# Full-array last tiles in an attention and DFT kernel: zero padding of keys, shift rows and DFT rows, and stores issued behind the next table's load

## The chip, the cores and the metric

The kernel runs on one core of a Trainium2 chip. The metric is the device time of one execution in microseconds (us), as the median of several executions. TensorE (PE) does the matrix products; its weight loads are shown apart as PEld. VectorE (DVE), ScalarE (ACT) and GpSimd (POOL) work on elements, and the SyncE queue (SP) issues most of the loads and stores.

## The reference

One encoder layer over 4096 tokens and 16 meta tokens put in front of them (4112 rows, model width 1024). After an RMS norm one projection gives the input of a Fourier branch, its gate, queries (8 heads of 64), keys and values (2 heads of 64) and an attention gate:

```
u = rmsnorm(h, norm_g)
f_in, f_gate, q, k, v, a_gate = split(u @ w_in)
f_out = (real(fft2(f_in over positions and 64 channels, ortho)) @ w_fmix + b_fmix) * silu(f_gate)
a_out = softmax(rope(norm(q)) @ rope(norm(k)).T / 8) @ v * silu(a_gate)
h = h + concat(f_out, a_out) @ w_out
out = rmsnorm(h, final_g)[16:]
```

All arithmetic is fp32 in the reference. The kernel reaches its accuracy with pairs of 16-bit numbers (a high part and a remainder), so that a projection takes three matmuls instead of one.

## The kernel before

**Phase A** (`phase_a`) makes the RMS statistics, the projections of 33 row tiles (tile 32, `NT`, holds the 16 meta rows), and the folded inputs of the position DFT. `proj` takes eight chunks of the model width, and for each the three products xh·wh, xh·wl and xl·wh (`mm3`, lines 84 to 86).

**Phase B** (`phase_b`) is the attention sweep. There are 8 blocks of 512 queries and 4 head pairs in each, so 32 "pairs" (b, p). A pair is a stream of 66 steps j: two heads times 33 key tiles. A step has two halves. `qk` multiplies one key tile with the 512 queries (L1031 the high part, L1032 the rest, in which the row shift sits as extra rows), ACT takes the exponential (L1035), and POOL or DVE subtracts its bfloat16 part (`rr`, L1037). `pvm`, four steps later, multiplies the probabilities with the values in nine matmuls (L1052 to L1059). In the last key tile of a head only 16 meta keys exist: `n = P if t < NT else NMETA`, so its two `qk` matmuls have 16 columns of weights and its nine `pvm` matmuls 16 rows. After it ACT copies the sum (L1063) and POOL does four operations on `ob` (L1067 to L1070).

Between the halves of the steps the sweep carries other work. Two matmuls with 64 rows per shift unit (`grp`, L962) find a row maximum for the next pair; DVE reduces them (L963). At step 63 `fin` (L993) transposes the shift row `nm`, 32 columns wide, and DVE spreads it into `qB` (L998) for the next pair. From the fifth pair on, the output projection of the block before (L1112) takes steps 14 to 61.

The position DFT is done in 17 units of 128 output rows for each of two parities (`dft_units`): 51 matmuls each, against a table `ct` of 1088 KB that `ct_load` fetches; the table pool has two buffers. Unit 16 holds the four rows left over, so its matmuls have four columns of weights, and its table of both parities is 68 KB. The first seven or so units run ahead of the sweep, up to 18 matmuls between two shift units (`f_step`); the others run inside the first pairs, three matmuls per step. A unit's end is `gather` (ACT copies the sum), and behind it `mix` applies the map and the gate; `mix` ends with POOL's product into `mo` (L869) and with the stores to `mf_d` (L872). While the first block runs, `block0` also fetches the output projection's weights (`wot`, L943) and splits them into `woh` (ACT) and `wol` (DVE), one chunk in seven steps from step `W0 = 234` on.

SP works in order: a store that waits for `mo` holds up every load written behind it. PE too takes its instructions strictly in the order in which they are written.

Of the kernel before, what the change touches and what calls it, by code (L numbers as in the profile page):

```python
# [32 lines left out]
P = 128  # L33
# [21 lines left out]
def emit(tc, a):  # L55
# [4 lines left out]
    with top:  # L60
# [39 lines left out]
        cts = []  # L100
# [26 lines left out]
def phase_a(tc, a, pool, mm3, id16, id32, sc):  # L127
# [15 lines left out]
    with ExitStack() as st:  # L143
# [150 lines left out]
        def proj(t, c0, c1):  # L294
# [3 lines left out]
            for d in range(ND):  # L298
                mm3(o, xh[:, d, :n], xl[:, d, :n], wh[:, d, c0:c1], wl[:, d, c0:c1], d == 0, d == ND - 1)
# [326 lines left out]
        wsplit(*GB, 3)  # L626
        tile_tr(NT)
        tile_gate(31, 768, fg_d)
# [43 lines left out]
def phase_b(tc, a, pool, mm3, id32, id16, sc):  # L672
# [10 lines left out]
    with ExitStack() as st:  # L683
# [14 lines left out]
        nm = [bp.tile([P, 32], F16, name=f"nm{i}") for i in range(2)]  # L698
# [60 lines left out]
        def dft_units(u, ty, spare):  # L759
# [3 lines left out]
            o, m = (0, P) if u < 16 else (4 * ty, 4)  # L763
# [3 lines left out]
            def one(*args):  # L767
# [4 lines left out]
                r = ps[0][:m, cs]  # L772
                if i == 8:
                    T.matmul(r, ct[0:96, x, 16, o:o + m], src[0:96, 8, 0, cs], start=False, stop=True,
                             skip_group_check=True)
                else:
                    T.matmul(r, ct[:, x, 2 * i + (w == 2), o:o + m], src[:, i, int(w == 1), cs],  # L777
# [5 lines left out]
            def gather():  # L783
                rows = slice(0, P) if u < 16 else slice(32 * ty, 32 * ty + 4)
                sk = stk if u < 16 else stk8
                c = ps[0][:m]
# [8 lines left out]
        behind = []  # L795
# [51 lines left out]
        def mix(u, early):  # L847
# [53 lines left out]
        def f_step(n, heavy, early=False):  # L901

            while flist:
# [49 lines left out]
        def max_units(i):  # L953
# [29 lines left out]
            def red():  # L983
                m = sm.tile([P, 4, 2], F32, tag="mm", name="mm")
                V.tensor_reduce(m, mx, axis=AX.X, op=ALU.max)
                V.scalar_tensor_tensor(out=n[:, 0:8].rearrange("p (e s)->p e s", s=4),
# [38 lines left out]
        def step(h, kv, t, qa, qb, acc, ob, gate):  # L1025
            n = P if t < NT else NMETA
            d = {}

            def qk(eng):
                s = pq.tile([P, 512], F32, tag="s", name="s")  # L1030
                T.matmul(s[:n], K[kv][:, t, 0, :n], qa, start=True, stop=False)  # L1031
                T.matmul(s[:n], K[kv][:, t, 1, :n], qb, start=False, stop=True)  # L1032
                pe = wk.tile([P, 512], F32, tag="pe", name="pe")
                rr = wk.tile([P, 512], F16, tag="rr", name="rr")
                S.activation(pe[:n], s[:n], AF.Exp, scale=HD ** -0.5)  # L1035
                hi = pe.bitcast(BF16)[:, 1::2]
                eng.tensor_tensor(out=rr[:n], in0=pe[:n], in1=hi[:n], op=ALU.subtract)  # L1037
                d["hi"], d["rr"] = hi, rr

            def pvm():  # L1040
# [6 lines left out]
                vh, va, vl = VV[:n, t, kv, :65], VV[:n, t, kv], VV[:n, t, kv, 65:129]  # L1047
# [415 lines left out]
```

## Time and profile before

| | |
|---|---|
| median of 3 runs | 3327.89 us (3327.48 to 3328.08) |
| profiled execution | 3325.33 us, of which the span shown is 3323.5 us |
| TensorE's granted clock, mean | 0.996 |
| PE busy | 3261.9 us (98%) |
| DVE, POOL, ACT busy | 71%, 68%, 51% |
| phase A, tables and first shift units, sweep | about 0 to 728, to 812, to the end |

A line of a timeline gives start, duration, engine, line, operation, output<-inputs and shape, and in brackets how long the engine was idle before and what released it. For matmuls "128\*16" is rows \* columns of the weights. Matmuls overlap in the pipeline: the distance from one start to the next says what a matmul costs, not the duration shown. A matmul streams its columns (512 in L1031) at 2.4 GHz when the granted clock is 1.00; 512 columns are 0.21 us.

### The profile page before, as it was taken

Reading aid. Unit: us, or ns where it says so; the run is one execution under the profiler, and the core shown is the slowest. Engines: PE = TensorE matmul, PEld = TensorE weight load, DVE = VectorE, ACT = ScalarE, POOL = GpSimd, SP = SyncE. Lnnn points to the kernel's source line nnn. Section 1 sums busy time; section 2 is a strip of 40 time slices with the busy share of each in tenths; the row PEclk is TensorE's granted clock in tenths of the full one; section 3 lists DMA queues with packets and bytes.
Section 4 is the critical chain, followed back from the end, with each engine's and each line's share of the span. In section 5 each row is a group of like instructions: output and inputs, shape, how many; then the busy total and the mean of one; then the engine's idle time right before and its main releaser. Section 6 shows DMA issues by size and latency. Waiting matters only on the chain.

```text
span 3323.5 us, 78632 instructions
## 1 busy us (share of the span) xinstructions
PE 3261.9 (98%) x33109; PEld 1888.5 (57%) x33109; DVE 2368.1 (71%) x3225; ACT 1703.8 (51%) x2967; POOL 2273.9 (68%) x2168
## 2 busy tenths in 40 slices
PE   8999999998999999999999999999999999999998
PEld 4555555556666555555555555555555555555554
DVE  6766565536666877777777777777777777777764
ACT  5443444333555555555555555555555555555553
POOL 3655555425777777777777777777777777777762
PEclk9999999999999999999999999999999999999999
DMA  6444444347422110110001000110100010000001
GB/s 220 145 164 134 140 150 133 102 151 212 131 91 65 66 53 23 36 45 21 21 21 46 21 20 24 49 33 21 46 21 21 20 46 21 24 29 28 21 21 58
DMA packets 142296, 223.58 MB, mean 67 GB/s; under 512 B 30358, under 2 KB 85478, under 8 KB 137590
## 3 DMA queue, kind: packets, MB, share of 16 engines
q1 hardware_dynamic: 128118, 193.38, 18.6%
q10 hardware_dynamic: 13824, 25.17, 2.0%
q8 instruction: 259, 4.24, 0.5%
q14 instruction: 95, 0.78, 0.1%
HBM read 157.38 MB, written 61.14 MB: 66 GB/s over the span
## 4 chain that ended last, share of the span: by engine, by line
PE 86%; POOL 5%; DVE 4%; DMA 2%; ACT 2%; issue 1%; SPq 0%; ACTq 0%; POOLq 0%; DVEq 0%
PE s L1031 13%; PE s L1032 12%; PE o L1052 11%; PE po L1112 9%; PE o L1059 7%; PE m L962 7%; PE ps L84 5%; PE ps L85 5%; PE ps L86 5%; POOL rr L1037 2%; PE pd L777 2%; PE o L1057 2%; PE o L1055 2%; PE m L1296 1%; PE pf L84 1%
## 5 line engine op out<-in xcount | busy, mean ns | idle before, releaser
L1037 POOL TENSOR_TENSOR rr<-pe 128x512 f16<-128x512 f32 x1572 | 1697.1, 1096 | 558.8 <-ACT pe L1035 551.2
L1035 ACT ACTIVATE pe<-s 128x512 f32<-128x512 f32 (+1 forms) x2112 | 1255.7, 596 | 1079.9 <-PE s L1032 995.8
L963 DVE TENSOR_REDUCE mx<-m 128x2 f32<-128x1024 f32 x1024 | 1206.6, 1220 | 307.8 <-PE m L962 305.2
L1059 PE MATMUL o<-VV,rr 128*128 128x65 f16 x8448 | 975.9, 193 | 6.4 <-POOL rr L1037 2.1
L1059 PEld LDWEIGHTS <-rr 128*128 128x128 f16 x8448 | 783.2, 98 | 176.6 <-POOL rr L1037 19.9
L1052 PE MATMUL o<-VV,pe 128*128 128x129 f16 x6336 | 849.6, 222 | 1.9 <-ACT tt L1063 1.9
L1052 PEld LDWEIGHTS <-pe 128*128 128x128 bf16 x6336 | 587.6, 97 | 396.4 <-issue 239.9
L1031 PE MATMUL s<-qA,K 128*128 128x512 f16 (+1 forms) x2112 | 800.3, 379 | 1.3 <-ACT pe L1035 1.3
L1032 PE MATMUL s<-qB,K 128*128 128x512 f16 (+1 forms) x2112 | 800.3, 379 | 0.8 <-DVE qB L998 0.8
L1037 DVE TENSOR_TENSOR rr<-pe 128x512 f16<-128x512 f32 x540 | 426.5, 790 | 218.4 <-ACT pe L1035 218.2
L1055 PE MATMUL o<-VV,pe 128*128 128x65 f16 (+1 forms) x2112 | 411.0, 195 | 0.0
L1057 PE MATMUL o<-VV,pe 128*128 128x64 f16 (+1 forms) x2112 | 410.4, 194 | 0.0
L84 PE MATMUL ps<-wh,xh 128*128 128x512 f16 (+2 forms) x1032 | 366.2, 355 | 8.4 <-ACT xh L287 8.3
L86 PE MATMUL ps<-wh,xl 128*128 128x512 f16 (+2 forms) x1032 | 366.0, 355 | 3.0 <-POOL xl L288 3.0
L85 PE MATMUL ps<-wl,xh 128*128 128x512 f16 (+2 forms) x1032 | 366.2, 355 | 0.1
L962 PE MATMUL m<-K,qP 64*128 64x512 f16 x2048 | 312.4, 382 | 4.9 <-DVE ml L1100 2.4
L1057 PEld LDWEIGHTS <-pe 128*128 128x128 bf16 (+1 forms) x2112 | 208.8, 99 | 0.0
L1031 PEld LDWEIGHTS <-K 128*128 128x128 f16 (+1 forms) x2112 | 202.5, 96 | 7.5 <-issue 0.4
L1055 PEld LDWEIGHTS <-pe 128*128 128x128 bf16 (+1 forms) x2112 | 206.2, 98 | 0.0
L1032 PEld LDWEIGHTS <-K 128*128 128x128 f16 (+1 forms) x2112 | 204.5, 97 | 2.0 <-issue 1.8
L962 PEld LDWEIGHTS <-qP 64*128 64x128 f16 x2048 | 59.6, 94 | 223.2 <-issue 221.5
L288 POOL TENSOR_TENSOR xl<-xt,xh 128x1024 f16<-128x1024 f32 (+1 forms) x33 | 68.7, 2082 | 150.1 <-ACT xh L287 150.1
(202 smaller groups left out, 3664.6 us busy)
## 6 DMA issues: line engine op xcount, KB each, us to landing
ct<-cd SPq DMA_DIRECT2D x16, 1088.0 KB
room<-x SPq DMA_DIRECT2D x32, 512.0 KB
xt<-xt SPq DMA_DIRECT2D x32, 512.0 KB
sg<-fx SPq DMA_DIRECT2D x16, 1024.0 KB
xr<-x SPq DMA_DIRECT2D x32, 512.0 KB
out<-yo SPq DMA_DIRECT2D x32, 512.0 KB
fg_d<-g ACTq DMA_DIRECT2D x32, 256.0 KB
ag_d<-g ACTq DMA_DIRECT2D x32, 256.0 KB
```

The source lines that it names most:

```text
L84: T.matmul(out, lh, rh, start=first, stop=False, skip_group_check=skip)
L85: T.matmul(out, lh, rl, start=False, stop=False, skip_group_check=skip)
L962: T.matmul(t[:, e], q[rs, s, p], K[kv][rs, 4 * c:4 * c + 4, 0], start=True, stop=True)
L963: V.tensor_reduce(mx[:, s, :, c], t, axis=AX.X, op=ALU.max)
L1031: T.matmul(s[:n], K[kv][:, t, 0, :n], qa, start=True, stop=False)
L1032: T.matmul(s[:n], K[kv][:, t, 1, :n], qb, start=False, stop=True)
L1035: S.activation(pe[:n], s[:n], AF.Exp, scale=HD ** -0.5)
L1037: eng.tensor_tensor(out=rr[:n], in0=pe[:n], in1=hi[:n], op=ALU.subtract)
L1052: T.matmul(o[:, c0:c0 + 129], hi[:n, cs], va, start=t == 0 and s == 0, stop=t == NT, skip_group_check=True)
L1055: T.matmul(o[:, c0:c0 + 65], hi[:n, cs], vh, start=False, stop=t == NT, skip_group_check=True)
L1057: T.matmul(o[:, c0:c0 + 64], hi[:n, cs], vl, start=False, stop=t == NT, skip_group_check=True)
L1059: T.matmul(o[:, c0:c0 + 65], rr[:n, cs], vh, start=False, stop=t == NT, skip_group_check=True)
```

## The change

Five edits that share one form:

- The last key tile uses 128 keys, of which 112 are zeros; the K and V tiles are cleared by POOL first, and `exp` and `rr` work on 128 rows.
- DFT unit 16 has a table with 128 columns, of which 124 are zeros, one of 1088 KB per parity; `gather` takes the first 4 rows.
- `nm` is 128 columns wide and `fin` transposes all of it.
- In the projection of keys and values the eight xl·wh products come after the sixteen others, and gate tile 31 comes ahead of the transposes of the meta tile.
- The stores of mapped rows are collected in `held` and issued by `release`, behind the next table's load, and at the end of the DFT behind `fgb` and the first two `wot` loads. `W0` is 240 instead of 234.

```diff
         def ct_load(u):
             if u < 16:
                 dma(ct, a["cd"][u])
             else:
-                dma(ct[:, :, :, 0:8], a["cdt"])
+                dma(ct, a["cdt"][len(done16)])
+                done16.append(None)
...
+                nc.gpsimd.memset(kk[0][:, NT, :, NMETA:], 0.0)
...
             for d in range(ND):
-                mm3(o, xh[:, d, :n], xl[:, d, :n], wh[:, d, c0:c1], wl[:, d, c0:c1], d == 0, d == ND - 1)
+                T.matmul(o, xh[:, d, :n], wh[:, d, c0:c1], start=d == 0, stop=False)
+                T.matmul(o, xh[:, d, :n], wl[:, d, c0:c1], start=False, stop=False)
+                if c0:
+                    T.matmul(o, xl[:, d, :n], wh[:, d, c0:c1], start=False, stop=d == ND - 1)
+            for d in range(ND if c0 else 0, ND):
+                T.matmul(o, xl[:, d, :n], wh[:, d, c0:c1], start=False, stop=d == ND - 1)
...
+        tile_gate(31, 768, fg_d)
         tile_tr(NT)
-        tile_gate(31, 768, fg_d)
...
-        nm = [bp.tile([P, 32], F16, name=f"nm{i}") for i in range(2)]
+        nm = [bp.tile([P, P], F16, name=f"nm{i}") for i in range(2)]
+        G.memset(K[1][:, NT, :, NMETA:], 0.0)
+        G.memset(VV[:, NT], 0.0)
...
-                    T.matmul(r, ct[:, x, 2 * i + (w == 2), o:o + m], src[:, i, int(w == 1), cs],
+                    T.matmul(r, ct[:, x, 2 * i + (w == 2)], src[:, i, int(w == 1), cs],
...
+        def release():
+            while held:
+                dma(*held.pop(0))
...
-                    dma(rows(mf_d, t0, m), mo[p0:p0 + m, ver])
+                    held.append((rows(mf_d, t0, m), mo[p0:p0 + m, ver]))
...
                     if fcur["later"] is not None:
                         ld["ct_load"](fcur["later"])
+                    release()
...
-                T.matmul(t[64:96, 0, :P], n, id16, start=True, stop=True)
+                T.matmul(t[:, 0, :P], n, id16, start=True, stop=True)
...
-                T.matmul(s[:n], K[kv][:, t, 0, :n], qa, start=True, stop=False)
-                T.matmul(s[:n], K[kv][:, t, 1, :n], qb, start=False, stop=True)
+                T.matmul(s, K[kv][:, t, 0], qa, start=True, stop=False)
+                T.matmul(s, K[kv][:, t, 1], qb, start=False, stop=True)
...
-                vh, va, vl = VV[:n, t, kv, :65], VV[:n, t, kv], VV[:n, t, kv, 65:129]
+                vh, va, vl = VV[:, t, kv, :65], VV[:, t, kv], VV[:, t, kv, 65:129]
...
-        W0 = 234
+        W0 = 240
...
                 wo_load(0)
                 wo_load(1)
+                release()
```

Which instructions stand in which order differs on SP in two places. The first is the queue in the early DFT, where `ct` is the next table, `mf_d<-mo` the stores of mapped rows and `fgu` the gate rows of a unit. Before:

```order
L872 DMA mf_d<-mo 121x512
L872 DMA mf_d<-mo 128x512
L105 DMA ct<-cd 128x4352
L845 DMA fgu<-fg_d 128x512 x2
L711 DMA qA_7749<-q_d 128x4x1024
L712 DMA qB_7751<-q_d 64x4x1024
L872 DMA mf_d<-mo 128x512 x2
L105 DMA ct<-cd 128x4352
```

And now:

```order
L105 DMA ct<-cd 128x4352
L807 DMA mf_d<-mo 121x512
L807 DMA mf_d<-mo 128x512
L857 DMA fgu<-fg_d 128x512 x2
L720 DMA qA_7750<-q_d 128x4x1024
L721 DMA qB_7752<-q_d 64x4x1024
L105 DMA ct<-cd 128x4352
L807 DMA mf_d<-mo 128x512 x2
```

Each table's load now stands ahead of the stores of the unit before, where it stood behind them; the gate rows are where they were.

The second place is the end of the DFT, where `wot` is the output projection's weights. Before:

```order
L872 DMA mf_d<-mo 128x512 x2
L872 DMA mf_d<-mo 4x512 x2
L872 DMA mf_d<-mo 3x512
L872 DMA mf_d<-mo 4x512
L1207 DMA fgb<-fgb 128x1024
L943 DMA wot<-wo 128x1024 x7
```

And now:

```order
L807 DMA mf_d<-mo 128x512 x2
L1219 DMA fgb<-fgb 128x1024
L956 DMA wot<-wo 128x1024 x2
L807 DMA mf_d<-mo 4x512 x2
L807 DMA mf_d<-mo 3x512
L807 DMA mf_d<-mo 4x512
L956 DMA wot<-wo 128x1024 x4
```

`fgb` and the first two weight chunks have moved ahead of the last four stores. On PE, DVE, ACT and POOL the sweep has the same instructions in the same order, with the last key tile's shapes changed from 16 to 128; the weight splits come six steps later, and POOL has the clearing of K, V and `nm` in addition.

## Rows read from the trace of the kernel before

**Rows 1.** The page's busy times of the engines, as shares of the span.

```profile
PE 3261.9 (98%) x33109; PEld 1888.5 (57%) x33109; DVE 2368.1 (71%) x3225; ACT 1703.8 (51%) x2967; POOL 2273.9 (68%) x2168
```

**Rows 2.** Four stretches: from:to, length, busy time of each engine (instructions), then the granted clock, the DMA share and GB/s.

```profile
775.00:779.00 4.00, 4.00 (x22) 2.40 (x21) 0.41 (x1) 0.87 (x2) 0.54 (x1) 0.57 0.70 215
1120.00:1177.00 57.00, 47.75 (x598) 27.74 (x596) 53.06 (x49) 35.19 (x57) 50.24 (x46) 1.00 0.29 95
1177.00:1182.00 5.00, 5.00 (x46) 3.02 (x44) 2.34 (x3) 1.79 (x3) 1.19 (x2) 0.66 1.04 302
2000.00:2800.00 800.00, 797.88 (x9084) 450.87 (x9085) 616.17 (x709) 445.37 (x752) 614.69 (x617) 1.00 0.11 31
```

**Rows 3.** The timeline of PE in the middle of a pair: two matmuls of an ordinary step, then the `qk` matmuls of the last key tile, and later its nine `pvm` matmuls, first and last.

```profile
2101.95 0.38 PE L1032 MATMUL s<-qB,K 128*128 128x512 f16 x1
2102.17 0.38 PE L1112 MATMUL po<-woh,ml 128*128 128x512 f16 x1
...
2102.71 0.19 PE L1059 MATMUL o<-VV,rr 128*128 128x65 f16 x1
2102.83 0.38 PE L1031 MATMUL s<-qA,K 128*16 128x512 f16 x1
2103.05 0.38 PE L1032 MATMUL s<-qB,K 128*16 128x512 f16 x1
2103.36 0.39 PE L1112 MATMUL po<-woh,mh 128*128 128x512 f16 x1
...
2108.02 0.38 PE L1112 MATMUL po<-wol,mh 128*128 128x512 f16 x1
2108.33 0.23 PE L1052 MATMUL o<-VV,pe 16*128 16x129 f16 x1
...
2108.67 0.19 PE L1059 MATMUL o<-VV,rr 16*128 16x65 f16 x1
2108.78 0.39 PE L1031 MATMUL s<-qA,K 128*128 128x512 f16 x1
```

**Rows 4.** The timeline of PE at the end of a pair: `fin` between two matmuls of the full form, and, seven steps later, a `pvm` that goes on only after a pause.

```profile
2139.33 0.38 PE L1032 MATMUL s<-qB,K 128*128 128x512 f16 x1
2139.75 0.23 PE L993 MATMUL m<-id,nm 128*32 128x128 f16 x1
2139.91 0.23 PE L1052 MATMUL o<-VV,pe 128*128 128x129 f16 x1
...
2150.93 0.23 PE L1052 MATMUL o<-VV,pe 128*128 128x129 f16 x1
2151.30 0.20 PE L1059 MATMUL o<-VV,rr 128*128 128x65 f16 x1
```

**Rows 5.** The timeline of POOL in the same stretch; consecutive instructions of one line are one row, and the four operations on `ob` that stand between the second and the third row, without a gap, are left out.

```profile
2141.22 5.02 POOL L1037 TENSOR_TENSOR rr<-pe 128x512 f16<-128x512 f32 x5 [0.48 <-ACT pe L1035]
2146.45 1.24 POOL L1037 TENSOR_TENSOR rr<-pe 128x512 f16<-128x512 f32 x1 [0.21 <-ACT pe L1035]
...
2149.75 4.48 POOL L1037 TENSOR_TENSOR rr<-pe 128x512 f16<-128x512 f32 x4
```

**Rows 6.** The timeline of PE in DFT unit 16: three matmuls with four columns of weights between two steps of the sweep.

```profile
828.33 0.38 PE L1032 MATMUL s<-qB,K 128*128 128x512 f16 x1
828.63 0.50 PE L777 MATMUL pd<-acs,ct 128*4 128x264 f16 x3
829.07 0.23 PE L1052 MATMUL o<-VV,pe 128*128 128x129 f16 x1
```

**Rows 7.** The costliest groups over the whole span with shapes kept apart: busy us, mean ns of one, idle time before.

```profile
L1037 DVE TENSOR_TENSOR rr<-pe 128x512 f16<-128x512 f32 x538 | 425.3, 791 | 218.1 <-ACT pe L1035 217.8
...
L1032 PEld LDWEIGHTS <-K 128*128 128x128 f16 x2048 | 198.9, 97 | 1.2 <-issue 1.1
...
L1037 POOL TENSOR_TENSOR rr<-pe 16x512 f16<-16x512 f32 x62 | 64.5, 1040 | 30.4 <-ACT pe L1035 30.3
...
L1032 PEld LDWEIGHTS <-K 128*16 128x16 f16 x64 | 5.6, 88 | 0.8 <-issue 0.8
```

**Rows 8.** The page of waits over the whole span (total us, times, longest), for PE on a table and for PE on POOL's `xl`.

```profile
PE pd L777 <- DMA ct<-cd: 7.8, 4, 2.4
PE ps L86 <- POOL xl L288: 3.0, 2, 2.0
```

**Rows 9.** The timeline of PE and of SP around one table in the early DFT: the last matmul of a unit's second half, the stores of the unit before and the load behind them, and the first matmul of the unit that reads that table.

```profile
749.76 0.27 PE L774 MATMUL pd<-acs,ct 96*128 96x248 f16 x1
...
752.82 0.74 SPq L872 DMA_DIRECT2D mf_d<-mo  x2
753.65 0.41 SPq L105 DMA_DIRECT2D ct<-cd  x1
...
762.17 1.07 PE L777 MATMUL pd<-acs,ct 128*128 128x264 f16 x8 [2.37 <-DMA ct<-cd]
```

**Rows 10.** The timelines of SP, ACT and PE at the end of the DFT: the last stores, the weights' loads behind them, the first split, and PE's longest pause there.

```profile
1100.93 17.48 SPq L872 DMA_DIRECT2D mf_d<-mo  x6
...
1123.37 1.06 ACT L947 ACTIVATE woh<-wot 128x1024 f16<-128x1024 f32 x1 [1.04 <-DMA wot<-wo]
...
1124.91 0.22 PE L1052 MATMUL o<-VV,pe 128*128 128x129 f16 x1 [1.74 <-ACT tt L1063]
```

**Rows 11.** The timeline of DVE: one `rr` that runs beside four operations of POOL on `ob`.

```profile
1161.28 2.62 DVE L1037 TENSOR_TENSOR rr<-pe 128x512 f16<-128x512 f32 x1
```

More of the change, by code (lines that the diff above doesn't have):

```diff
@@ L98, in acs_load @@
             acs[ty] = t
-        cts = []
+        cts, done16 = [], []
         def ct_load(u):
@@ L762, in dft_units @@
             ct, src = ld["cts"].pop(0), ld["acs"][ty]
-            o, m = (0, P) if u < 16 else (4 * ty, 4)
             mms = []
@@ L771, in one @@
                 cs = slice(0, NC_) if x == 0 else slice(NC_, 512)
-                r = ps[0][:m, cs]
+                r = ps[0][:, cs]
                 if i == 8:
-                    T.matmul(r, ct[0:96, x, 16, o:o + m], src[0:96, 8, 0, cs], start=False, stop=True,
+                    T.matmul(r, ct[0:96, x, 16], src[0:96, 8, 0, cs], start=False, stop=True,
                              skip_group_check=True)
                 else:
-                    T.matmul(r, ct[:, x, 2 * i + (w == 2), o:o + m], src[:, i, int(w == 1), cs],
+                    T.matmul(r, ct[:, x, 2 * i + (w == 2)], src[:, i, int(w == 1), cs],
                              start=i == 0 and w == 0, stop=False, skip_group_check=True)
@@ L785, in gather @@
                 sk = stk if u < 16 else stk8
-                c = ps[0][:m]
+                c = ps[0][:P if u < 16 else 4]
                 S.activation(sk[rows, :, 0:64], c[:, 0:256].rearrange("p (g c)->p g c", g=4), AF.Copy, scale=FNORM)
@@ L793, in dft_units @@
             return [(lambda z=z: one(*z)) for z in mms], gather
-        behind = []
+        behind, held = [], []
+        def release():
+            while held:
+                dma(*held.pop(0))
         def catch_up():
@@ L985, in red @@
                 V.tensor_reduce(m, mx, axis=AX.X, op=ALU.max)
-                V.scalar_tensor_tensor(out=n[:, 0:8].rearrange("p (e s)->p e s", s=4),
+                V.scalar_tensor_tensor(out=n[:, 64:72].rearrange("p (e s)->p e s", s=4),
                                        in0=m.rearrange("p s e->p e s"), scalar=-1.0 / 256.0,
@@ L1025, in step @@
         def step(h, kv, t, qa, qb, acc, ob, gate):
-            n = P if t < NT else NMETA
             d = {}
@@ L1030, in qk @@
                 s = pq.tile([P, 512], F32, tag="s", name="s")
-                T.matmul(s[:n], K[kv][:, t, 0, :n], qa, start=True, stop=False)
-                T.matmul(s[:n], K[kv][:, t, 1, :n], qb, start=False, stop=True)
+                T.matmul(s, K[kv][:, t, 0], qa, start=True, stop=False)
+                T.matmul(s, K[kv][:, t, 1], qb, start=False, stop=True)
                 pe = wk.tile([P, 512], F32, tag="pe", name="pe")
                 rr = wk.tile([P, 512], F16, tag="rr", name="rr")
-                S.activation(pe[:n], s[:n], AF.Exp, scale=HD ** -0.5)
+                S.activation(pe, s, AF.Exp, scale=HD ** -0.5)
                 hi = pe.bitcast(BF16)[:, 1::2]
-                eng.tensor_tensor(out=rr[:n], in0=pe[:n], in1=hi[:n], op=ALU.subtract)
+                eng.tensor_tensor(out=rr, in0=pe, in1=hi, op=ALU.subtract)
                 d["hi"], d["rr"] = hi, rr
@@ L1051, in pvm @@
                     if s < 3:
-                        T.matmul(o[:, c0:c0 + 129], hi[:n, cs], va, start=t == 0 and s == 0, stop=t == NT,
+                        T.matmul(o[:, c0:c0 + 129], hi[:, cs], va, start=t == 0 and s == 0, stop=t == NT,
                                  skip_group_check=True)
                     else:
-                        T.matmul(o[:, c0:c0 + 65], hi[:n, cs], vh, start=False, stop=t == NT,
+                        T.matmul(o[:, c0:c0 + 65], hi[:, cs], vh, start=False, stop=t == NT,
                                  skip_group_check=True)
-                        T.matmul(o[:, c0:c0 + 64], hi[:n, cs], vl, start=False, stop=t == NT,
+                        T.matmul(o[:, c0:c0 + 64], hi[:, cs], vl, start=False, stop=t == NT,
                                  skip_group_check=True)
-                    T.matmul(o[:, c0:c0 + 65], rr[:n, cs], vh, start=False, stop=t == NT, skip_group_check=True)
+                    T.matmul(o[:, c0:c0 + 65], rr[:, cs], vh, start=False, stop=t == NT, skip_group_check=True)
                 if t == NT:
@@ L1375, in shape_constants @@
     cd = np.zeros((16, P, 2, 17, P), f16)
-    cdt = np.zeros((P, 2, 17, 8), f16)
+    cdt = np.zeros((2, P, 2, 17, P), f16)
     for odd in range(2):
@@ L1389, in shape_constants @@
                 cd[2 * u + odd, :, x] = full[:, :, u * P:(u + 1) * P]
-            cdt[:, x, :, 4 * odd:4 * odd + 4] = full[:, :, NM:]
+            cdt[odd, :, x, :, :4] = full[:, :, NM:]
     j = np.arange(NTOK)
```

## The prediction, made before the changed kernel ran

> **What bounds the kernel now.** Read the page's busy times first: PE is busy 98% of the span, the other engines 51 to 71% [rows 1]. Then the stretches: in the middle of the sweep PE is busy 797.88 of 800 us at a granted clock of 1.00 [rows 2]. So no wait to speak of is left there, and time can only come out of what PE does while it counts as busy. That is why the next view is PE's timeline, read from start to start. In an ordinary step L1112 starts 0.22 us after L1032: the 512 columns take 512/2400 = 0.21 us, and hardly anything comes on top. After the 65 columns of an L1059 the next matmul would start 65/2400 = 0.03 us later. Around the last key tile these distances are longer: 0.12 into the 16-column matmul instead of 0.03, 0.31 out of it instead of 0.22, 0.31 into the 16-row matmul, 0.11 out of it [rows 3]. Between matmuls of the same narrow form nothing is lost. So PE pays about 0.09 us each time the form of its weights changes, four times per last tile: 0.36 us. Outside the steady sweep two stretches have real waits: the tables before the sweep (7.8 us in four waits [rows 8]) and the end of the DFT, where PE is busy 47.75 of 57 us [rows 2].
>
> **The change part by part.**
>
> *Last key tiles, steady sweep* (27 pairs, the fifth to the 31st). Each pair has two such tiles and one `fin`. In the middle of the pair the tile's `rr` is ready early, so its 0.36 us is gained in full. At the end it is different. `fin` costs 0.42 - 0.22 = 0.20 going in, where it may also wait for DVE's `nm`, and 0.16 - 0.06 = 0.10 coming out [rows 4]; with the second tile that makes 0.66 us on paper. But POOL is the engine that is late there: its rows run from 2141.22 with one gap of 0.21 us up to 2154 [rows 5], and PE's `pvm` at 2150.93 goes on only at 2151.30 [rows 4], 0.37 instead of the usual 0.06: it waits for POOL's `rr`. What PE saves at the end of a pair it then waits longer there, except for what also moves POOL forward: the exit of the 16-column tile lets the next exponentials start about 0.1 us sooner, into the 0.21 us gap. So a pair gains 0.36 + 0.10 = 0.46 us, and 27 pairs 12.4 us. The upper bound is everything, 0.36 + 0.66 = 1.02, times 27 is 27.5; the lower is 0, if the pauses are not due to the form. I take 12.4 since the POOL rows have no room. What the padding adds costs nothing here: `rr` on 16 rows took 1040 ns [rows 7] against the 5.02 / 5 = 1.00 us of a full one [rows 5], and a weight load 88 against 97 ns [rows 7], which lies beside the matmul ahead of it.
>
> *The first four pairs*: DFT matmuls stand between their steps in place of the output projection, so PE is slower there and POOL less late; I take 0.68 of the 1.02, times 4 is 2.7 us, between 0 and 4.1. *The last pair*: 0.3 us.
>
> *DFT unit 16*: three matmuls in a step go in with 0.30 instead of 0.22 and out after 0.44, where three times 264 columns take 0.33 [rows 6]: about 0.1 either way. The two units' 102 matmuls are 34 groups; all but one go out into the full form, and about 24 come from it (the others follow a 64-row matmul, whose own switches stay). 57 x 0.096 = 5.5 us, between 0 and 6.5. PE has no slack to wait for there. The tables grow by 1020 KB each; at the 215 GB/s of 775 to 779 [rows 2] that is some 5 us of transfer, and a table is asked for a whole unit ahead, more than 20 us inside the sweep.
>
> *Early tables*: the load at 753.65 stands in SP's queue behind stores that wait for `mix` (752.82), although its buffer came free when the unit ended at 749.76 [rows 9]. It lands too late: PE waits 2.37 us at 762.17. Issued at the unit's end, each such load comes some 3 us sooner, more than the longest wait of 2.4, so the four waits go: 7.8 us [rows 8]. One of them also has an after-effect. Behind the second wait, from 775 to 779, PE's granted clock is 0.57 [rows 2], near the lower of the levels 1.2 and 2.4 GHz; 4 us x 0.43 = 1.7 us of lost clock. Together 9.5 us. From below 1.5 (if the transfers, not the queue, are the limit), from above 10.2 (a little more of the half clock). The stores, now behind the load, are late for nobody: `mf` is read from the fifth pair on. The gate rows `fgu` still stand behind the stores, as before.
>
> *End of the DFT*: the six stores hold SP for 17.48 us from 1100.93; the weights come behind them, ACT waits 1.04 us for them with the exponentials queued behind, and PE loses 1.74 us at 1124.91 [rows 10]. With the loads ahead and the splits six steps later, this wait goes. The rest of the 9.25 us that PE idles from 1120 to 1177 is DVE's (busy 53.06 of 57 [rows 2]), and its work is only moved: one split falls behind the start of the output projection instead of before it. The stretch from 1177 to 1182 at clock 0.66 [rows 2] loses 1.7 us that may go or stay. I take 3.5 us, 1.74 and a share of the others, between -2 (a split that collides with the projection) and 8.
>
> *Head of phase A*: PE waits 3.0 us in two places for `xl` [rows 8], the product that the new order puts last in the key and value projection. DVE's preparation of the weights bounds most of this stretch, so I take 0.5 us, between -2 (gate tile 31 ahead of the transposes may leave PE idle on its weights) and +2. *Clearing* K, V and `nm` on POOL lies before the sweep, beside the early DFT: 0.
>
> **Sum**: 12.4 + 2.7 + 0.3 + 5.5 + 9.5 + 3.5 + 0.5 = 34.4 us. The profiled execution took 3325.33 us, 2.56 less than the median of the runs. 3325.33 - 34.4 + 2.6 = 3293.5, say 3293 us.
>
> **A rule that speaks against it.** The trace shows 88 ns for a load of 16 columns of weights and 97 ns for 128 [rows 7]. The Trainium skill, page "TensorE: Matmul & The Clock Gate", section "LDWEIGHTS (loading the stationary operand)", says that a load's time goes with its columns, at 1.2 columns per ns. By it, as an estimate, 16 columns take 13 ns and 128 take 107, and the 262 loads that are widened (102 in the DFT, 128 of K, 32 of `nm`) would add up to some 25 us if none were hidden, so that the kernel would come out near 3318. The trace does not agree for narrow loads.
>
> **The rivals.**
> (a) *POOL does not hold the pair's end back.* If DVE's `rr` and the gap give way, the steady pairs gain 1.02 each: 15.1 us more, 3278. For it: the pause is one or two `pvm` long and the gap of 0.21 exists. Against it: POOL's rows are otherwise without a break [rows 5].
> (b) *The tables are bound by the transfers.* 70% of DMA time is taken from 775 to 779 [rows 2]; a load asked for earlier then lands hardly earlier, and 1.5 remains of 9.5: 3301. Against it: the share is not full, and DMA is idle between a table's landing and the next store.
> (c) *The pauses are not due to the form* (an address change, another accumulator). Then the padding gives nothing: 34.4 less 20.9 leaves 13.5, 3314. Against it: four different narrow matmuls show the same 0.09, and their likes of full form do not [rows 3, 6].
> (d) *Slower: DVE and POOL get in each other's way.* One `rr` on DVE took 2.62 us [rows 11] beside POOL's four operations at a pair's end, some 1.8 more than the mean of 0.79 [rows 7]. If PE's new phase brings that meeting into every steady pair and PE waits for it, 27 x 1.8 = 49 us come back: 3342. It decides from 34.4 / 27 = 1.3 us per pair on. For it: neither engine has slack there. Against it: the phase moves by 0.4 us of 75. The Trainium skill, page "SBUF — State Buffer", section "Who interferes with whom", has DVE and GpSimd exclude each other on one shared port pair for whole instructions; the 2.62 us agrees with that.
> (e) *Wider weight loads show.* By the rows 262 x 9 ns = 2.4 us: 3296.
>
> **How the numbers follow.** The forecast 0.62, (a) 0.15, (b) 0.12, (c) 0.04, (d) 0.04, (e) 0.03. The forecast's own bounds come from the end of the DFT (+5.5 and -4.5), the head (+2.5, -1.5) and the tables; they give 3285 to 3301. (a) lies below at 3278, (b) above at 3301; with the loss of some of DFT unit 16 the upper end becomes 3306. The range 3277 to 3306 leaves out (c), (d), and half of (a). A measurement of this kernel can tell 0.2%, 6.7 us, from no change. All cases but (d) are faster by more than that; I leave 0.04 for a half of them cancelled by something unseen: faster 0.92, same 0.04, slower 0.04.
>
> **What would show it.** Start-to-start distances of 0.03 and 0.22 us around the last key tile and 0.33 for three DFT matmuls of unit 16: right; 0.12 and 0.31 again: (c). No row of PE waiting for a table before the sweep, and a clock of 1.00 from 770 to 779. The pair's pause at its fourth step longer than 0.37 by about 0.5 us, with POOL unbroken ahead of it: the absorption is right; no longer pause: (a). The period of a steady pair falls by 0.46 us. The prediction is wrong if that period falls by nothing, or if a new wait for DVE's or POOL's `rr` appears in every pair.

## The result, and the profile after

The changed kernel takes 3295.41 us (median of 4 runs, 3292.66 to 3297.37), against 3327.94 for the one before: a ratio of 0.9902, with a 95% interval of 0.9885 to 0.9919. 3293 was forecast, with a range of 3277 to 3306. Beside the later experiments the kernel before took 3323 to 3325 us, and three kernels whose steady pairs are as long as the changed one's (x_nm32, x_w234, x_head) 3296 to 3297, so the gain is 27 to 33 us. The profiled execution is the fastest of the four, 3292.66 us with a span of 3290.9. All working below is between this one and the profiled execution of before, 32.7 us apart.

The page's busy times hardly changed their shares, as one expects where the gain is time in which PE counted as busy [rows 1]:

```profile
PE 3223.4 (98%) x33109; PEld 1896.5 (58%) x33109; DVE 2379.2 (72%) x3225; ACT 1699.1 (52%) x2967; POOL 2280.2 (69%) x2171
```

PE has 38.5 us less to do with the same 33109 matmuls, and 5.9 us more in which it waits. So the stretches of [rows 2] read differently now (from:to, length, busy time of PE, PEld, DVE, ACT and POOL, clock, DMA share, GB/s):

```profile
775.00:779.00 4.00, 4.00 (x42) 3.10 (x40) 2.10 (x3) 1.88 (x5) 2.66 (x2) 1.00 0.05 10
2000.00:2800.00 800.00, 793.48 (x9138) 454.12 (x9137) 626.48 (x728) 447.38 (x759) 616.43 (x621) 1.00 0.10 30
```

The half clock at 775 is gone, and so is the one from 1177 on: from 748 to 3284 us the mean granted clock is 1.00. In the steady sweep PE idles 6.52 of 800 us where it idled 2.12 before: part of what it saved has become a wait.

The timeline of PE around the last key tile, in the middle of a pair, answers to [rows 3]:

```profile
2151.51 0.19 PE L1071 MATMUL o<-VV,rr 128*128 128x65 f16 x1
2151.54 0.38 PE L1043 MATMUL s<-qA,K 128*128 128x512 f16 x1
2151.76 0.38 PE L1044 MATMUL s<-qB,K 128*128 128x512 f16 x1
2151.97 0.38 PE L1124 MATMUL po<-woh,mh 128*128 128x512 f16 x1
...
2156.62 0.38 PE L1124 MATMUL po<-wol,mh 128*128 128x512 f16 x1
2156.84 0.22 PE L1064 MATMUL o<-VV,pe 128*128 128x129 f16 x1
...
2157.17 0.19 PE L1071 MATMUL o<-VV,rr 128*128 128x65 f16 x1
2157.20 0.38 PE L1043 MATMUL s<-qA,K 128*128 128x512 f16 x1
```

0.03, 0.21, 0.22 and 0.03 us from start to start, where 0.12, 0.31, 0.31 and 0.11 stood. DFT unit 16 likewise [rows 6]: 0.22 us into the three matmuls and 0.34 over them, the 3 x 264 columns at 2.4 GHz and no more.

```profile
816.30 0.38 PE L1044 MATMUL s<-qB,K 128*128 128x512 f16 x1
816.52 0.50 PE L785 MATMUL pd<-acs,ct 128*128 128x264 f16 x3
816.86 0.22 PE L1064 MATMUL o<-VV,pe 128*128 128x129 f16 x1
```

At the end of a pair [rows 4] the way out of `fin` takes 0.06 instead of 0.16 us. The way in is still 0.42, so that was a wait for `nm`, which DVE (L999) finishes at 2413.24, 0.06 us ahead of it. And the pause between the first two matmuls of `pvm` at step 4 has grown from 0.37 to 0.70:

```profile
2412.88 0.38 PE L1044 MATMUL s<-qB,K 128*128 128x512 f16 x1
2413.30 0.23 PE L1006 MATMUL m<-id,nm 128*128 128x128 f16 x1
2413.36 0.22 PE L1064 MATMUL o<-VV,pe 128*128 128x129 f16 x1
...
2424.15 0.23 PE L1064 MATMUL o<-VV,pe 128*128 128x129 f16 x1
2424.85 0.20 PE L1071 MATMUL o<-VV,rr 128*128 128x65 f16 x1 [0.47 <-POOL rr L1049]
```

The waits of PE from 1300 to 2900 us name the releaser (total, times, longest); this stretch of before has no such line at all. By the prediction's last sentence a new wait for `rr` in every pair would prove it wrong; this one is the pause of before made longer, which it forecast:

```profile
PE o L1071 <- POOL rr L1049: 9.7, 22, 0.5
```

POOL's timeline there [rows 5] has lost its gap of 0.21 us: from 2414.77 it works without a break.

```profile
2414.77 6.48 POOL L1049 TENSOR_TENSOR rr<-pe 128x512 f16<-128x512 f32 x6 [0.48 <-ACT pe L1047]
...
2423.31 6.92 POOL L1049 TENSOR_TENSOR rr<-pe 128x512 f16<-128x512 f32 x6
```

In the early DFT the loads now go first [rows 9], and of four waits of 7.8 us [rows 8] one of 1.08 is left:

```profile
756.52 0.27 PE L782 MATMUL pd<-acs,ct 96*128 96x248 f16 x1
756.63 1.06 PE L785 MATMUL pd<-acs,ct 128*128 128x264 f16 x8
...
756.82 0.33 SPq L105 DMA_DIRECT2D ct<-cd  x1
759.86 0.80 SPq L807 DMA_DIRECT2D mf_d<-mo  x2
...
768.06 1.52 PE L785 MATMUL pd<-acs,ct 128*128 128x264 f16 x12 [1.08 <-DMA ct<-cd]
```

The load is issued 0.3 us after the unit's end, and the table is there 11.2 us later; before, one took 8.5. So the queue no longer holds the load back; how near the transfers are to their limit then was not tried.

Where the 32.7 us came from can be read by landmarks that both traces have: the last matmul of the first DFT half (L774, L782) and the first score matmul (L1031, L1043) of each pair, read from the timelines of PE.

| stretch | before | after | gained | forecast |
|---|---|---|---|---|
| to the end of the first DFT half | 731.67 | 728.95 | 2.72 | 0.5 |
| from there to the first pair | 80.19 | 70.90 | 9.29 | 9.5 |
| pairs 1 to 5 | 425.85 | 416.25 | 9.6 | 12.2 |
| pairs 6 to 31 (26) | 1959.18 | 1948.73 | 10.45, 0.40 each | 12.0, 0.46 each |
| last pair and what follows | 126.65 | 126.04 | 0.60 | 0.3 |

### The profile page after: what moved, and what is told of

The parts are those of the page before. It is cut to its first block, busy times and chain, and to the rows that moved or that the text cites. A ratio compares the mean times of both kernels' runs of the same rounds, so it can differ in the third digit from the quotient of the medians.

```text
span 3290.9 us, 78633 instructions
## 1 busy us (share of the span) xinstructions
PE 3223.4 (98%) x33109; PEld 1896.5 (58%) x33109; DVE 2379.2 (72%) x3225; ACT 1699.1 (52%) x2967; POOL 2280.2 (69%) x2171
## 4 chain that ended last, share of the span: by engine, by line
PE 85%; POOL 5%; DVE 4%; ACT 2%; issue 2%; DMA 1%; SPq 0%; ACTq 0%; POOLq 0%; DVEq 0%
PE s L1043 12%; PE s L1044 12%; PE o L1064 11%; PE po L1124 9%; PE m L975 7%; PE o L1071 7%; PE ps L302 5%; PE ps L301 5%; PE ps L304 4%; POOL rr L1049 3%; PE pd L785 2%; PE o L1069 2%; PE o L1067 2%; ACT pe L1047 1%; PE m L1309 1%
## 5 line engine op out<-in xcount | busy, mean ns | idle before, releaser
L1047 ACT ACTIVATE pe<-s 128x512 f32<-128x512 f32 x2112 | 1257.2, 597 | 1066.1 <-PE s L1044 1002.6
L1043 PE MATMUL s<-qA,K 128*128 128x512 f16 x2112 | 799.0, 378 | 3.9 <-ACT pe L1047 1.9
L1044 PE MATMUL s<-qB,K 128*128 128x512 f16 x2112 | 799.7, 379 | 1.8 <-DVE qB L1011 0.9
L1064 PEld LDWEIGHTS <-pe 128*128 128x128 bf16 x6336 | 591.4, 97 | 360.9 <-issue 191.5
L1049 DVE TENSOR_TENSOR rr<-pe 128x512 f16<-128x512 f32 x540 | 445.9, 826 | 222.7 <-ACT pe L1047 219.4
L1067 PE MATMUL o<-VV,pe 128*128 128x65 f16 x2112 | 411.4, 195 | 0.0
L1069 PE MATMUL o<-VV,pe 128*128 128x64 f16 x2112 | 410.4, 194 | 0.0
L302 PE MATMUL ps<-wl,xh 128*128 128x512 f16 (+2 forms) x1032 | 352.5, 353 | 7.3 <-DVE wl L272 7.3
L304 PE MATMUL ps<-wh,xl 128*128 128x512 f16 x768 | 291.8, 380 | 0.0
L1044 PEld LDWEIGHTS <-K 128*128 128x128 f16 x2112 | 205.0, 97 | 7.4 <-issue 7.3
L1069 PEld LDWEIGHTS <-pe 128*128 128x128 bf16 x2112 | 209.1, 99 | 0.0
L1067 PEld LDWEIGHTS <-pe 128*128 128x128 bf16 x2112 | 206.5, 98 | 0.0
L1043 PEld LDWEIGHTS <-K 128*128 128x128 f16 x2112 | 203.5, 96 | 0.8 <-issue 0.4
```

The source lines that it names most:

```text
L302: T.matmul(o, xh[:, d, :n], wl[:, d, c0:c1], start=False, stop=False)
L1043: T.matmul(s, K[kv][:, t, 0], qa, start=True, stop=False)
L1044: T.matmul(s, K[kv][:, t, 1], qb, start=False, stop=True)
L1047: S.activation(pe, s, AF.Exp, scale=HD ** -0.5)
L1049: eng.tensor_tensor(out=rr, in0=pe, in1=hi, op=ALU.subtract)
L1064: T.matmul(o[:, c0:c0 + 129], hi[:, cs], va, start=t == 0 and s == 0, stop=t == NT, skip_group_check=True)
```

## The experiments

Each undoes or adds one thing to the changed kernel. Times of executions of one kernel lie 2 to 10 us apart, while in the traces the steady pairs hardly differ (see the end), and the kernel before took 3323 to 3325 us beside them, so times are given with their ratio to it and the verdicts rest on periods: the time from the first score matmul of one pair to that of the next, equal within some 0.02 us for equal pairs. In the changed kernel most steady pairs have 74.72 us, before 75.11.

**The last key tile at 16 keys again** (x_tile16)

```diff
+            n = P if t < NT else NMETA
...
-                T.matmul(s, K[kv][:, t, 0], qa, start=True, stop=False)
+                T.matmul(s[:n], K[kv][:, t, 0, :n], qa, start=True, stop=False)
...
-                vh, va, vl = VV[:, t, kv, :65], VV[:, t, kv], VV[:, t, kv, 65:129]
+                vh, va, vl = VV[:n, t, kv, :65], VV[:n, t, kv], VV[:n, t, kv, 65:129]
```

> The changed kernel with the last key tile back at 16 keys (all else as changed). Theory (a change of the weights' form costs PE about 0.09 us): the period of a steady pair goes up by 0.40 us, all of what the change took from it (75.11 against 74.72 us in most pairs), the distances around the last key tile are 0.12 and 0.31 us again, and the time is about 3295 + 26 x 0.40 + some 3 for the first pairs and the last, 3308 to 3309 us. Rival (the steady gain has another cause, such as nm or the new place of the loads): the period stays at 74.7 and the time at 3295.

Measured: 3310.6 us (0.9963 of before, 0.9948 to 0.9977), and 75.12 us per pair, 0.40 to 0.41 more in nearly every steady pair. The pause at step 4 is back at 0.34 us (mean over 25 pairs; 0.67 in the changed kernel). The whole gain of the steady sweep is the last key tile's.

**Padded to 64 keys** (x_tile64), the same edit with 64 in place of `NMETA`.

> As changed, but the last key tile padded to 64 keys only (64 columns of weights, 64 rows). Theory (any form but the full one costs the same at its borders): as with 16 keys, period 75.1, distances 0.12 and 0.31 us, time 3308 us. Rival (what is lost grows with the part of the array that is left out): 64 of the 112 rows and columns are still left out, so a bit over half, period 74.95, time 3302 us.

Measured: 3310.82 us (0.9962, 0.9949 to 0.9974), 75.15 us per pair. A tile half as wide loses as much as one of 16. Its timeline shows the same steps, 0.12 in and 0.31 out:

```profile
2160.80 0.19 PE L1073 MATMUL o<-VV,rr 128*128 128x65 f16 x1
2160.92 0.40 PE L1045 MATMUL s<-qA,K 128*64 128x512 f16 x1
2161.16 0.38 PE L1046 MATMUL s<-qB,K 128*64 128x512 f16 x1
2161.47 0.39 PE L1126 MATMUL po<-woh,mh 128*128 128x512 f16 x1
```

So the price is one of the change between forms and not of the part left out.

**Only the value half at 16 rows** (x_pv16)

```diff
-                vh, va, vl = VV[:, t, kv, :65], VV[:, t, kv], VV[:, t, kv, 65:129]
+                vh, va, vl = VV[:m, t, kv, :65], VV[:m, t, kv], VV[:m, t, kv, 65:129]
```

with `m` the 16 rows of the last tile, and `hi[:m]`, `rr[:m]` for the other side.

> As changed, but only the value half of the last key tile back at 16 rows; its score half stays at 128 columns. Theory: two of the four changes of form come back, 0.18 us per pair in the middle of a pair, and at the end of a pair nothing more, since PE waits for POOL there: period 74.9, time about 3295 + 27 x 0.18 + 1 = 3301 us. If the end of a pair absorbs nothing: 0.36 per pair, 3306. If the cost sits in the narrow score columns alone: 3295.

Measured: 3303.28 us (0.9943, 0.9928 to 0.9957), 74.93 us per pair, 0.21 more: two changes of form per tile, once per pair. The second tile of the pair pays them too, but the pause at step 4 falls from 0.67 to 0.45 us at the same time. That is the absorption seen directly.

**`nm` at 32 columns** (x_nm32)

```diff
-        nm = [bp.tile([P, P], F16, name=f"nm{i}") for i in range(2)]
+        nm = [bp.tile([P, 32], F16, name=f"nm{i}") for i in range(2)]
...
-                T.matmul(t[:, 0, :P], n, id16, start=True, stop=True)
+                T.matmul(t[64:96, 0, :P], n, id16, start=True, stop=True)
```

> As changed, but nm back at 32 columns. Theory (PE waits for POOL behind a pair's end, so a saving there is absorbed): fin costs 0.3 us more again, PE's pause at the fourth step of the next pair gets shorter by nearly that, period 74.7 to 74.76, time 3295 to 3297 us. Rival (the end of a pair is not held back): 0.2 to 0.3 us per pair, 3301 to 3304 us.

Measured: 3296.68 us (0.9922, 0.9907 to 0.9936), 74.71 us per pair: the width of `nm` is worth nothing. But the pause at step 4 is 0.67 us as in the changed kernel, not shorter, so POOL is not what takes up this saving. The scores of steps 63, 64 and 65 show what is; first this kernel, then the changed one:

```profile
2416.53 0.38 PE L1043 MATMUL s<-qA,K 128*128 128x512 f16 x1
...
2417.70 0.38 PE L1043 MATMUL s<-qA,K 128*128 128x512 f16 x1
...
2418.61 0.38 PE L1043 MATMUL s<-qA,K 128*128 128x512 f16 x1
```
```profile
2412.66 0.38 PE L1043 MATMUL s<-qA,K 128*128 128x512 f16 x1
...
2413.72 0.38 PE L1043 MATMUL s<-qA,K 128*128 128x512 f16 x1
...
2414.74 0.38 PE L1043 MATMUL s<-qA,K 128*128 128x512 f16 x1
```

1.17 and 0.91 us against 1.06 and 1.02. The 0.1 us of `fin` is back one step later, because the score buffer of step 65 comes free only when ACT is through with step 63, and ACT has its square (L1141) in front of that (ACT's timeline in the changed kernel):

```profile
2413.06 1.05 ACT L1141 ACTIVATE xr<-hh 128x1024 f32<-128x1024 f32 x1
...
2414.10 1.08 ACT L1047 ACTIVATE pe<-s 128x512 f32<-128x512 f32 x2
```

**DFT unit 16 with four columns** (x_dft4)

```diff
-                    T.matmul(r, ct[:, x, 2 * i + (w == 2)], src[:, i, int(w == 1), cs],
+                    T.matmul(r, ct[:, x, 2 * i + (w == 2), :P if u < 16 else 4], src[:, i, int(w == 1), cs],
...
```

> As changed (wide tables of 1088 KB included), but the matmuls of DFT unit 16 use 4 columns of weights again. Theory (form): the first and the fourth pair, in which the two units run, get longer by 2.5 to 2.9 us each, the rest of the sweep by nothing; time about 3295 + 5.5 = 3301 us. Rival (the gain of these pairs comes from the loads or from the last key tiles alone): no pair longer by over 0.5, 3295.

Measured: 3302.8 us (0.9941, 0.9925 to 0.9958). The first pair is 2.79 us longer, the fourth 3.54 and the fifth 0.54; the second and third not by 0.01. Of the 4.08 us in the fourth and fifth some 1.3 are not the price of the narrow matmuls. From 1141.7 to 1145.1, late in the fourth pair, the granted clock is 0.50 here, the lower of the levels 1.2 and 2.4 GHz, and 1.00 in the changed kernel. But the kernel n_rr63 below, which has the same instructions as the changed one up to the end of the fifth pair, wide matmuls included, shows such a stretch late in its fourth pair too, and its fourth and fifth pair are 0.56 and 0.72 us longer:

```profile
1137.70:1141.10 3.40, 3.40 (x24) 2.05 (x23) 2.33 (x5) 1.19 (x2) 1.53 (x2) 0.50 0.00 0
```

That leaves 2.8 us for the second unit (when its last group is through, at step 20, the fourth pair is 2.9 us behind), and the wide matmuls gain 5.6 in all, where 5.5 was forecast.

**Stores ahead of the next table again** (x_rel)

```diff
-                    held.append((rows(mf_d, t0, m), mo[p0:p0 + m, ver]))
+                    dma(rows(mf_d, t0, m), mo[p0:p0 + m, ver])
```

> As changed, but the mapped rows are stored at once again, ahead of the next table's load. Theory: the early DFT gets its waits for tables back, four of 1.4 to 2.4 us, and a stretch at half clock; the stretch from the first DFT unit to the first step of the sweep grows from 70.9 by 8 to 9.5 us, to about 80, and the end of the DFT (fourth and fifth pair) by some 2; time about 3306 us. Rival (the tables were late for another reason, which the padding took away): 3295.

Measured: 3307.09 us (0.9948, 0.9933 to 0.9963). From the first DFT half to the first pair 80.41 us instead of 70.90, and 1.3 us more in the fourth and fifth pair, which again have a stretch at clock 0.50 (1144.2 to 1147.6). As n_rr63 loses as much there with the stores behind the load, no cost of the order is shown in these two pairs. The waits from 730 to 820 us have the tables again:

```profile
PE pd L785 <- DMA ct<-cd: 7.0, 4, 2.6
```

Where the first and the last of these waits end (761.82 and 806.59), stretches of 3.4 us at clock 0.50 begin, at 761.9 and 806.3, as the expectation had it. The order on SP alone is worth 9.5 us there, the whole gain of that stretch; in the twelve traces with the loads first it takes 69.8 to 72.3 us.

**W0 at 234** (x_w234)

> As changed, but the splits of the output weights begin at step 234 again. Theory: the weights are there in time now, so only the load of DVE decides; the splits lie seven to six steps earlier, one more of them before the output projection's first stage: the fourth and fifth pair together change by -1 to +1 us, 3294 to 3296. Rival (the later start is what removed the wait): the fourth pair longer by 2 to 4 us, 3298.

Measured: 3296.62 us (0.9919, 0.9904 to 0.9934); the fourth pair is 0.72 us shorter and the fifth 2.99 longer, 2.27 together. Neither expectation fits: 2.27 lies outside the -1 to +1, and it is the fifth pair that gets longer, not the fourth. A weight split of DVE and PE's pause behind it in the fifth pair's timelines, in this kernel and then in the changed one:

```profile
1157.36 1.22 DVE L961 SCALAR_TENSOR_TENSOR wol<-wot,woh 128x1024 f16<-128x1024 f32 x1 [3.02 <-ACT woh L960]
...
1159.77 0.39 PE L975 MATMUL m<-K,qP 64*128 64x512 f16 x2 [2.05 <-DVE ml L1112]
```
```profile
1154.36 1.23 DVE L961 SCALAR_TENSOR_TENSOR wol<-wot,woh 128x1024 f16<-128x1024 f32 x1 [2.11 <-ACT woh L960]
...
1156.77 0.39 PE L975 MATMUL m<-K,qP 64*128 64x512 f16 x2 [0.78 <-DVE ml L1112]
```

`ml` is an input of the output projection's first stage, and DVE has the weight split in front of it in both; here it waits longer for ACT. But PE's idle time in the whole fifth pair is only 0.2 us longer (3.86 against 3.63), since other waits are shorter; its busy time is 2.8 us longer (77.6 against 74.8) with the same matmuls. That is the clock: two stretches of 3.4 us at 0.50, from 1149.9 and from 1160.2 on, the second 0.4 us behind the end of the wait for `ml`. The changed kernel has none there.

```profile
1160.20:1163.60 3.40, 3.40 (x24) 2.02 (x24) 1.78 (x2) 0.60 (x1) 1.31 (x2) 0.50 0.90 257
```

The kernel before, with `W0` at 234 too, waits 2.43 us for `ml` until 1176.44 and has its half clock behind that, from 1177.8 on. Whether the clock falls there in every execution, one trace of each kernel does not show.

**The head's old order** (x_head): `mm3` in the key and value projection, gate tile 31 behind the transposes.

> As changed, but the key and value projection and gate tile 31 in their old order. Theory (DVE's preparation of the weights bounds the head): the start of the first DFT unit moves by less than its scatter between runs (728.9 to 732.5 us so far), time 3294 to 3297. Rival (PE's shorter wait for xl counts): the first unit starts later, at 732 to 734, time 3297 to 3299 us.

Measured: 3296.2 us (0.9921, 0.9907 to 0.9936), first DFT half ending at 730.89 us, inside the scatter. PE's waits from 0 to 700 us, with the old order and then with the new:

```profile
PE ps L303 <- POOL xl L290: 3.2, 3, 2.0
PE kt L384 <- DVE ks L377: 2.8, 1, 2.8
...
PE ps L302 <- DVE wl L272: 1.2, 4, 0.4
```
```profile
PE ps L302 <- DVE wl L272: 7.3, 5, 4.9
...
PE ps L306 <- POOL xl L290: 0.7, 2, 0.5
```

The two waits that the new order removes, 3.2 and 2.8 us, come back as a wait for DVE's weights, 7.3 instead of 1.2.

**What holds PE behind a pair's end.** Three kernels take a piece out of that run. The first puts the `rr` of step 63 on DVE (n_rr63).

```diff
-            on_dve = {j + 2 for j in AT}
+            on_dve = {j + 2 for j in AT} | ({63} if i > 3 else set())
```

> As changed, but the rr of step 63 goes to DVE instead of POOL from the fifth pair on, so POOL has one of 1.04 us less in its unbroken run across the end of a pair. Theory (POOL's run is what PE waits for at the fourth and fifth step, 0.67 and 0.26 us where 0.06 is usual): both pauses go, up to 0.8 us per pair, period 73.9 to 74.2, time 3272 to 3282 us; DVE's reductions of the row maxima come 0.7 us later. Rival (PE is held there by something else, or DVE's delay takes its place): period 74.6 or more, time 3293 or more.

Measured: 3326.92 us (1.0009, 0.9999 to 1.0018), 75.82 us per pair: 1.11 us slower, which takes back about as much as the change had gained. DVE's and PE's timelines show why:

```profile
2439.04 0.69 DVE L1049 TENSOR_TENSOR rr<-pe 128x512 f16<-128x512 f32 x1 [1.48 <-ACT pe L1047]
2439.76 1.22 DVE L1011 TENSOR_TENSOR qB<-m,id 8x1024 f16<-8x1024 f32 x1
...
2441.04 0.38 PE L1044 MATMUL s<-qB,K 128*128 128x512 f16 x1 [0.82 <-DVE qB L1011]
```

The `rr` waits 1.48 us for its exponential, and `qB`, which the next pair's first score needs, stands behind it on DVE. The new wait comes ahead of the old one, and the row maxima behind it are late as well.

The second puts the `rr` of step 4, the one that PE waits for, on DVE (n_rr4): `| ({4} if i > 4 else set())` in the same line.

> As changed, but the rr of step 4, the one that PE waits for, goes to DVE from the sixth pair on; POOL goes from its four operations on ob straight to step 5. Theory: as with step 63, the two pauses go, up to 0.8 us per pair, period 73.9 to 74.2, time 3273 to 3283 us. Rival (DVE is no earlier with it, since it reduces row maxima from 2420.4 to 2422.7): the pause stays, period 74.7, time 3295 or more.

Measured: 3283.88 us (0.9877, 0.9863 to 0.9892), 74.15 us per pair: 0.56 us faster per pair than the changed kernel. Both pauses at steps 4 and 5 are gone. What remains of the 0.8 is a wait at step 8:

```profile
2415.51 1.02 DVE L1049 TENSOR_TENSOR rr<-pe 128x512 f16<-128x512 f32 x1 [0.31 <-ACT pe L1047]
2416.45 2.34 DVE L976 TENSOR_REDUCE mx<-m 128x2 f32<-128x1024 f32 x2
...
2418.35 0.89 PE L975 MATMUL m<-K,qP 64*128 64x512 f16 x4
```

In the changed kernel the next matmul starts 0.53 us after the first of these four; here it starts at 2419.17, 0.82 us after, as the second two wait for the buffer that DVE's maxima of step 4 leave at 2418.79.

The third moves ACT's square behind step 63 into the next pair, to step 5 (n_sq).

```diff
-                    prev[0]()
+                    if i + 1 == len(pairs):
+                        prev[0]()
...
+                if prev and j in (5, 9):
+                    prev[j == 9]()
```

> As changed, but ACT's square of the finished rows (1.05 us, between the exponentials of steps 62 and 63) and the root behind it are done in the next pair at steps 5 and 9. Theory (POOL's run starts when the exponential of step 63 lets it, 0.75 us late because of the square, and the scores of step 65 wait for the same exponential): POOL's run begins 0.5 to 0.75 us earlier and PE's pauses shrink by as much, period 74.0 to 74.3, time 3275 to 3288 us. Rival (the run's start is set by POOL itself): 3295.

Measured: 3291.86 us (0.9901, 0.9884 to 0.9917), 74.58 us per pair: 0.14 gained of the 0.5 to 0.75 expected. POOL is early as expected: counted from the pair's first score it is through with the `rr` of step 4 at 8.53 us instead of 9.27. Of the 0.74, 0.29 are an earlier start, and 0.45 come because this `rr` takes 1.04 us here and 1.49 in the changed kernel, where it starts while an `rr` of DVE is still running (the kernel before has about as much there). PE's pauses fall from 0.67 to 0.07 and from 0.26 to 0.09 us. But the square now delays the exponential of step 6, for which PE loses 0.5 us ahead of the first pause, and at step 14 another 0.37 go to a longer wait for DVE's `ml`. The first of the two:

```profile
2426.55 0.38 PE L1043 MATMUL s<-qA,K 128*128 128x512 f16 x1 [0.35 <-ACT pe L1047]
```

The last run exchanges steps 4 and 6 between POOL and DVE (n_rr4for6).

```diff
+            if i > 4:
+                on_dve = (on_dve - {6}) | {4}
```

> As n_rr4 (the rr of step 4 on DVE from the sixth pair on), and in exchange the rr of step 6 on POOL, so that DVE has no more to do than in the changed kernel. Theory: in n_rr4 PE lost 0.3 us per pair again behind DVE's later row maxima (from 0.8 to 0.56 gained); with the exchange DVE is on time, POOL has its rr of step 6 between steps 5 and 7, where PE needs the later ones 1.1 to 1.5 us after they are ready: period 73.9 to 74.1, time 3274 to 3281 us. Rival (POOL, one instruction longer behind the pair's end, is late at step 6 instead of 4): period 74.2 to 74.6, time 3284 to 3293.

Measured: 3281.34 us (0.9872, 0.9856 to 0.9889), 74.15 us per pair, the same as n_rr4 in every pair. Neither 73.9 to 74.1 nor the rival's 74.2 to 74.6: POOL is not late at step 6, but the 0.3 us at step 8 stays, since it hangs on the maxima of step 4, which stand behind the `rr` of step 4 and ahead of that of step 6. Nobody waited for DVE's `rr` of step 6. This and n_rr4 are the fastest versions, some 1.2% below the kernel before; their medians differ by less than their runs scatter.

## Why the prediction was right, and where its terms were off

The time, 3295.4, is 2.4 us above the forecast 3293. The sum of 34.4 us stands against 32.7 between the two traces and 32.5 between the medians. That it comes so near is in part luck: 2.7 of the 32.7 us lie in the head, where they are scatter, and the 2.2 of them that were not forecast make up for over half of the 4 us that the rest gained less. Term by term:

**Form changes in the steady sweep: right, size 0.40 instead of 0.46.** "Four times per last tile: 0.36 us" is shown by x_tile16, and x_tile64 and x_pv16 show that it is the change of form that costs: half the array costs the same as an eighth, and half of the changes cost half. Rival (c) falls. The Trainium skill, page "TensorEngine Tiling (Array Packing)", section "Key Properties", says that changing the tiling mode drains TensorE. No run shows a mode or a drain as such; what fits is the 0.09 to 0.10 us at each change between a full matmul and one of 64 or fewer rows or columns. The prediction's "each time the form of its weights changes" is too wide: the DFT's matmuls of 96 rows (L782) cost nothing at either border. The one shown above takes 0.11 us from start to start for 248 columns (248/2400 = 0.10), and the medians of all 36 are 0.003 us more than the columns need on the way in and 0.007 on the way out. The step that was mis-sized is "what also moves POOL forward ... about 0.1 us": POOL's gap closed, but it gave only 0.40 - 0.36 = 0.04.

**Absorbed at a pair's end: right, by two engines instead of one.** Forecast was a pause at step 4 longer by about 0.5 us; it grew by 0.32, from 0.35 to 0.67 as means over 25 pairs. That is the second last tile's 0.36 less the 0.04. The saving of `fin` is taken up earlier, at the scores of step 65 behind ACT's square (x_nm32), which the prediction did not see; nor that 0.2 us of `fin` was a wait for `nm` throughout, so that a pair had 0.82 us to save and not 1.02. For the sum it made no difference. Rival (a), that the end does not hold back, falls with x_nm32 and x_pv16. n_rr4 shows the other side: with one `rr` less on POOL both pauses go and 0.56 us per pair come out; in n_sq POOL is 0.74 us earlier and the pauses go too, but PE waits elsewhere instead.

**Early tables: right** (9.29 against 9.5, and x_rel 9.5, half clock behind the waits included). Of the waits 6.7 us went and 1.08 stayed; the half clock at 775 went. Rival (b) was partly right: between 748 and 770 us the DMA share is 0.92 where it was 0.72, and one load took 11.2 us.

**Pairs 1 to 5: 9.6 against 12.2.** Singly undone, unit 16 is worth 5.6 us (forecast 5.5) and the last tiles 2.4 (x_tile16: 0.35, 0.83, 0.50, 0.42 and 0.31; forecast 2.7 + 0.46). That leaves 1.6 for the end of the DFT, where 3.5 was forecast: this is the term that was mis-sized. Its reason, "1.74 and a share of the others" of PE's waits, did not hold. Here are the fourth and fifth pair together, before and then now:

```profile
1073.50:1237.70 164.20, 154.75 (x1785) 86.53 (x1783) 129.50 (x131) 91.51 (x158) 124.60 (x120) 0.99 0.20 60
```
```profile
1057.30:1216.10 158.80, 149.40 (x1785) 89.11 (x1782) 130.04 (x131) 91.65 (x158) 124.55 (x120) 1.00 0.20 62
```

PE idles 9.45 us before and 9.40 now. The 1.74 us behind ACT's `tt` went and the wait for `ml` fell from 2.43 to 0.78, but PE now waits 1.4 us longer for DVE's maxima and 0.9 for `qB`, which it did not wait for before. What is gone there is the half clock at 1177, which the prediction left open. By x_w234 `W0` alone is worth 2.3 us, so the parts add up to 10.3 against 9.6; where the 0.7 between them goes was not tried.

**Head: no gain shown.** The 2.72 us between the two traces are scatter. In the twelve traces with the new order the first DFT half ends between 728.95 and 732.88 us, 731.4 on average; the kernel before ended at 731.67 and x_head, with the old order, at 730.89. No gain can be told, and the waits show a trade.

**Rival (d)** did not come with the change: the longest `rr` on DVE from 1300 to 2900 us takes 1.56 us and the median 0.69. The 2.62 us of [rows 11] were read wrongly: POOL was still at its own `rr` until 1162.83 and then did the first two operations on `ob`, not four. n_rr63 is slower by another way, an exponential that DVE waits for, and does not bear on (d). A small meeting of that kind is in every pair before and after, the 1.49 us of POOL's `rr` at step 4 (n_sq). **Rival (e)**, wider weight loads: PEld's busy time grew by 8.0 us, but no distance from start to start shows it: the padded matmuls start as close to each other as full ones did.

## What to carry to other kernels

Where an engine is at 98%, read its timeline from start to start and compare with what the columns need: a lone matmul of 64 or fewer rows or columns among full ones pays at both borders, and padding it with zeros is free as long as its loads and element work stand beside other work. Before adding up such savings over a period, find the waits inside it: a saving ahead of a wait whose releaser does not move is lost, and this one lost 0.4 of 0.8 us per pair that way. And before giving a difference between two traces to an edit, look whether both had the same granted clock: one stretch of 3.4 us at half clock made the fourth and fifth pair of n_rr63 1.3 us longer, ahead of anything that its edit moves. An in-order queue is worth reading for what stands ahead of the critical load: 9.5 us here came from letting stores go second.

## What the runs showed of the hardware that was not expected

A weight tile of 64 columns or rows costs at its borders as much as one of 16: 0.43 us per pair against 0.40; one of 96 rows costs nothing there. Stretches of 3.4 us at half clock come in some traces and not in others whose instructions are the same up to there (n_rr63 and n_sq have one late in the fourth pair; the changed kernel and n_rr4 do not). The stretch ahead of the first DFT unit, which has the same instructions in twelve kernels, differed by 3.9 us between executions, and the first pair by up to 1.7 us, as PE waited up to 1.8 us there for a load (`acs`, L96) to land. The steady pairs behind them agree within some 0.02 us each in kernels with the same sweep; two versions can be told apart in the sweep that their total times cannot tell apart.
